# Second context normed in the second mixer, inverse and down products put off, four buffers for the context branch's split weights, later transposes

## The chip, the cores and the metric

The kernel runs on one core of one Trainium2 chip. The metric is the device time of one execution in microseconds (us), as a median over runs. TensorE (PE) multiplies matrices, VectorE (DVE), ScalarE (ACT) and GpSimd (POOL) do the elementwise work, SyncE (SP) issues most of the transfers and POOL the rest; each of these engines works through its own instructions in a fixed order.

## What is computed

`first_block` runs two layers over 256 latent tokens `x` and 256 context tokens `ctx` of 1024 channels, and `second_block` runs a hyena layer and an attention layer over the resulting latent tokens and over a second context `ctx_2`. All matrices are fp32, and nearly all weights are used once. Cut to what matters here:

```
for l in range(2):                      # first_block
    mod   = silu(c) @ w_ada[l] + b_ada[l]          # 6 vectors per stream
    x     = x + gt1 * (token_mixer(norm(x)) @ w_out[l])
    x     = x + gt2 * expert_choice_ffn(norm(x))   # 16 experts, 32 tokens each:
                                                   # (silu(xs@w_gate) * (xs@w_up)) @ w_down
    # ctx the same, in layer 0 alone
for s, t in ((x_lat, c), (ctx_2, c_ctx_2)):        # second_block, layer 0: hyena
    sh, sc, gt = split(silu(t) @ ada_w_2[0] + ada_b_2[0], 3)
    h = rms_norm(s) * (1 + sc) + sh
    x0, x1, v, z = h @ hy_w_in                     # x0, x1, v through a short conv
    u = x1 * v
    y = (irfft(rfft(u) * rfft(k)) + u * d) * x0    # long convolution
    s = s + gt * ((y * silu(z)) @ hy_w_out)
x = x + gt * attention(norm(x), norm(ctx_2))       # layer 1, modulated by ada_w_2[1]
```

## The kernel before

The kernel is written in a tile language whose scheduler decides the order of the instructions on each engine from the order of the code, the dependences and the number of buffers of each tag. The program passes through these stages, in the times of the profiled execution: mixer 0 and routing (0 to 400 us), the 16 experts of layer 0 (to 880), mixer 1 (to 1101; its inner core ends at 1046 and its output projection, on the tiles `mhi` and `mlo`, follows), routing of layer 1 (to 1140), then the 16 experts of layer 1 with the hyena layer of the second context beside them, and from 1835 the latent hyena (to 2080) and attention (to 2365).

**Weights and splitting.** A weight comes in tiles of 1 MB. Expert weights (`ew`) and the modulation weights (`ada`) are used as they are. The weights of projections and of the hyena layer are split by `split` into a high part `hi` (a CAST on ACT) and a low part `lo` (a subtraction on DVE), 512 columns at a time, and each product is made of three matmuls (`mm3`, L109 to L111: hi by hi, lo by hi, hi by lo). `hi` and `lo` have `self.sbufs` buffers each, 2 until the latent hyena.

**Modulation.** `ada` computes the modulation vectors (PE L191; columns L198) from weight tiles of 1 MB that rotate through the five `W` buffers. A table `PLACES` says at which place of the program which step stands, so "1" is w_ada of layer 1 and "a" and "b" are ada_w of the second block's two layers; a place that is in `EVERY` puts its steps between pieces of the mixer's core (`beside`), and the others run their steps in one go.

**Experts of layer 1.** Each of the 16 experts has 12 tiles of 1 MB (four each of gate, up and down), 192 in all, 16 matmuls each (PE L823, inputs `XS` for gate and up, `hT` for down). The first six go to a tag `W2` of their own, the others to the `W` buffers. An expert runs gate, up, `h` (ACT L851, DVE L854), transposes of `h` (L857), down, and `Y` (DVE L869).

**Context hyena.** It stands behind the experts in the code with PSUM of its own, and the scheduler interleaves the two. The context `ctx_2` is loaded, normed and transposed (PE L244) into `hyx`. Then 15 blocks of 128 channels follow (the 16th comes after the step `between`). A block has two weight tiles `Wb` (POOL issues them, two buffers), four projections of 8 by 3 matmuls on `hyx`, convolutions (ACT L1048, DVE L1049 to L1053), a sum and difference `uf` on POOL (L1058) and its transposes on PE (L1059, copied to `u`), a forward transform (`psm<-u,fe`, L1017), the product with the filter `Kt` on DVE (`Yf`, L1075 to L1077), an inverse transform (`ptp<-fi,Yf`, L1017), the product `x0s` (DVE L1088), and its split into `hmh` and `hml`. After every four blocks the output projection (`out_proj`) runs on `hmh` and `hml`.

## Time and profile before

| | |
|---|---|
| median of 3 runs | 2364.46 us (2359.9 to 2367.83) |
| profiled execution | 2366.99 us, span 2365.2 us |
| granted TensorE clock, mean | 0.955 |
| PE busy | 2135.7 us (90%) |
| DVE, ACT, POOL busy | 53%, 31%, 8% |
| DMA | 664.09 MB, mean 281 GB/s |

The span is the profiled time from the first to the last instruction. A busy share is a mean over the whole span, and the stages have different limits, so it says little about one stage. Idle time of an engine that is not the bottleneck costs nothing. A row that names a releaser ("<-DVE lo") says what ended the idle time ahead of the instruction.

### The profile page before, as it was taken

Reading aid. Unit: us, or ns where it says so; the run is one execution under the profiler, and the core shown is the slowest. Engines: PE = TensorE matmul, PEld = TensorE weight load, DVE = VectorE, ACT = ScalarE, POOL = GpSimd, SP = SyncE. Lnnn points to the kernel's source line nnn. Section 1 sums busy time; section 2 is a strip of 40 time slices with the busy share of each in tenths; the row PEclk is TensorE's granted clock in tenths of the full one; section 3 lists DMA queues with packets and bytes.
Section 4 is the critical chain, followed back from the end, with each engine's and each line's share of the span. In section 5 each row is a group of like instructions: output and inputs, shape, how many; then the busy total and the mean of one; then the engine's idle time right before and its main releaser. Section 6 shows DMA issues by size and latency. Waiting matters only on the chain.

```text
span 2365.2 us, 35049 instructions
## 1 busy us (share of the span) xinstructions
PE 2135.7 (90%) x13966; PEld 1436.1 (61%) x13966; DVE 1250.4 (53%) x2533; ACT 737.5 (31%) x1414; POOL 187.7 (8%) x315
## 2 busy tenths in 40 slices
PE   5999988999999989998799998898777999999998
PEld 3776664343343436864376766665234999979786
DVE  3954444333433337654355555544125878875776
ACT  3323331000000014343233222222013555555665
POOL 1000000011010100000011011100001110100100
PEclk8999999999999999999899999998777999999999
DMA  8247545999999996459799999988996545435320
GB/s 342 99 157 312 204 184 193 413 415 415 414 413 415 414 405 251 137 194 370 295 351 365 372 374 370 351 336 327 421 421 262 185 144 188 168 132 189 126 81 26
DMA packets 129588, 664.09 MB, mean 281 GB/s; under 512 B 12666, under 2 KB 23429, under 8 KB 62352
## 3 DMA queue, kind: packets, MB, share of 16 engines
q1 hardware_dynamic: 115616, 602.89, 66.0%
q0 software_dynamic: 13808, 58.96, 6.6%
q8 instruction: 110, 1.80, 0.3%
q14 instruction: 54, 0.44, 0.1%
HBM read 656.56 MB, written 5.24 MB: 280 GB/s over the span
## 4 chain that ended last, share of the span: by engine, by line
PE 72%; DVE 9%; issue 8%; DMA 7%; ACT 3%; POOL 1%; SPq 0%; DVEq 0%; POOLq 0%; ACTq 0%
PE pmm L823 16%; PE pmm L109 12%; PE pmm L111 11%; PE pmm L110 11%; PE pad L191 3%; PE psm L875 2%; DMA W<-in_w_e_gate 1%; DVE lo L105 1%; DMA W<-in_w_e_up 1%; PE ptp L1017 1%; DMA W<-in_w_ada 1%; PE pmm L798 1%; PE pad L978 1%; DMA W<-in_ada_w 1%; PE ppo L1247 1%
## 5 line engine op out<-in xcount | busy, mean ns | idle before, releaser
L823 PE MATMUL pmm<-W,XS 128*32 128x256 f32 (+1 forms) x3040 | 378.8, 478 | 39.7 <-DMA W<-in_w_e_gate 20.3
L105 DVE TENSOR_TENSOR lo<-W,hi 128x512 fp32r<-128x512 f32 (+1 forms) x420 | 283.7, 680 | 187.1 <-ACT hi L104 184.2
L104 ACT CAST hi<-W 128x512 fp32r<-128x512 f32 (+1 forms) x420 | 255.5, 612 | 352.0 <-PE pmm L110 162.9
L823 PEld LDWEIGHTS pmm<-W,XS 128*32 128x32 f32 (+1 forms) x3040 | 127.0, 123 | 241.3 <-issue 151.1
L823 PE MATMUL pmm<-W,hT 128*32 128x256 f32 (+1 forms) x1536 | 190.1, 483 | 20.2 <-DVE hT L101 8.3
L111 PE MATMUL pmm<-hyx,lo 128*128 128x256 f32 x640 | 191.6, 299 | 10.6 <-DVE lo L105 10.6
L109 PE MATMUL pmm<-hyx,hi 128*128 128x256 f32 x640 | 193.4, 302 | 4.8 <-ACT hi L104 4.8
L110 PE MATMUL pmm<-hyx,hi 128*128 128x256 f32 x640 | 185.8, 290 | 0.0
L105 DVE TENSOR_TENSOR lo<-Wb,hi 128x512 fp32r<-128x512 f32 x160 | 109.4, 692 | 117.3 <-ACT hi L104 116.3
L104 ACT CAST hi<-Wb 128x512 fp32r<-128x512 f32 x160 | 96.8, 619 | 209.4 <-PE pmm L110 138.3
L869 DVE TENSOR_TENSOR Y<-pmm,gt 32x512 f32<-32x512 f32 (+1 forms) x128 | 70.9, 554 | 143.5 <-PE pmm L823 141.8
L109 PE MATMUL pmm<-hyl,hi 128*128 128x256 f32 x512 | 144.5, 283 | 1.7 <-DVE rtmp L697 1.7
L110 PE MATMUL pmm<-hyl,hi 128*128 128x256 f32 x512 | 144.1, 282 | 0.0
L111 PE MATMUL pmm<-hyl,lo 128*128 128x256 f32 x512 | 143.1, 283 | 0.0
L109 PEld LDWEIGHTS pmm<-hyx,hi 128*128 128x128 f32 x640 | 126.6, 198 | 23.7 <-ACT hi L104 16.6
L111 PEld LDWEIGHTS pmm<-hyx,lo 128*128 128x128 f32 x640 | 126.3, 197 | 22.3 <-DVE lo L105 14.1
L823 PEld LDWEIGHTS pmm<-W,hT 128*32 128x32 f32 (+1 forms) x1536 | 65.6, 125 | 117.6 <-issue 68.6
L110 PEld LDWEIGHTS pmm<-hyx,hi 128*128 128x128 f32 x640 | 126.6, 198 | 2.4 <-issue 2.2
L851 ACT ACTIVATE h<-pmm 128x256 f32<-128x256 f32 (+1 forms) x31 | 15.1, 488 | 362.1 <-PE pmm L823 361.9
L191 PE MATMUL pad<-W,cpad 128*32 128x512 f32 x576 | 91.0, 643 | 21.6 <-DMA W<-in_w_ada 16.7
L854 DVE TENSOR_TENSOR h<-h,pmm 128x512 f32<-128x512 f32 (+1 forms) x32 | 17.7, 552 | 171.9 <-ACT h L851 89.5
L109 PEld LDWEIGHTS pmm<-hyl,hi 128*128 128x128 f32 x512 | 97.4, 190 | 3.4 <-issue 1.9
(516 smaller groups left out, 4084.1 us busy)
## 6 DMA issues: line engine op xcount, KB each, us to landing
W<-in_w_e_gate SPq DMA_DIRECT2D x128, 1024.0 KB, 11.2
W<-in_w_e_up SPq DMA_DIRECT2D x128, 1024.0 KB, 11.2
W<-in_w_e_down SPq DMA_DIRECT2D x128, 1024.0 KB, 11.2
W<-in_w_ada SPq DMA_DIRECT2D x48, 1024.0 KB, 6.6
W<-in_hyw SPq DMA_DIRECT2D x32, 1024.0 KB, 5.1
Wb<-in_hyw POOLq DMA_DIRECT2D x30, 1024.0 KB, 8.9
W<-in_ada_w SPq DMA_DIRECT2D x24, 1024.0 KB, 5.2
W<-in_at_w_in SPq DMA_DIRECT2D x16, 1024.0 KB, 5.0
```

What stands on the lines that cost most here:

```text
L104: self.nc.scalar.copy(hi, w)
L105: self.nc.vector.tensor_tensor(lo, w, hi.bitcast(F32), op=OP.subtract)
L109: mm(out, lhsT=l[0], rhs=r[0], start=start, stop=False)
L110: mm(out, lhsT=l[0], rhs=r[1], start=False, stop=False)
L111: mm(out, lhsT=l[1], rhs=r[0], start=False, stop=stop)
L191: nc.tensor.matmul(ps[32 * j:32 * j + 32, :], lhsT=self.cpad[:, blk, k0 + k, :], rhs=wt[:, k, j * 512:(j + 1) * 512], start=(k0 + k == 0), ...
L798: nc.tensor.matmul(ps, lhsT=v, rhs=S[s][:, t], start=(t == 0 and q == 0), stop=(t == 1 and q == 1))
L823: self.nc.tensor.matmul(ps[M * j:M * j + M], lhsT=v, rhs=wt[:, j * N:(j + 1) * N], start=(k == 0), stop=(k == 7))
L869: nc.vector.tensor_tensor(Y[s][32 * r:32 * r + 32, c], py[p0:p0 + 32], gt[s][p0:p0 + 32, c], op=OP.mult)
L875: nc.tensor.matmul(ps, lhsT=SgT[s][:, q, t * 128:(t + 1) * 128], rhs=Y[s][:, n * 512:(n + 1) * 512], start=True, stop=True)
L978: nc.tensor.matmul(ps[:, i, f], lhsT=self.fd[:, t, i * 256 + f * 128:i * 256 + (f + 1) * 128], rhs=ab[:, i, t], start=(t == 0), stop=(t == 1))
L1017: self.nc.tensor.matmul(out, lhsT=l[0], rhs=r[0], start=start, stop=stop)
```

## The change

1. The steps "a1 b0 b1" of `ada` move from the place R1 (routing of layer 1) to L1 (beside the pieces of the second mixer's core). Tiles of the second mixer that had room for both streams have room for the latent one alone.
2. `ctx_2` is loaded, normed and transposed right behind the second mixer, in place of behind the experts.
3. The split weights have four buffers, in place of two, in the context hyena (two again during `between`).
4. In the context hyena a block's inverse transform, the product `x0s` and the output projection are put off until the next block has made `uf` (`pend`, `flush`, `back`). The transposes of `uf` stand behind the third projection, in place of directly behind `uf`. `Yf` and `x0s` get two buffers.
5. With one stream, an expert's down products (`down`, from the transposes of `h` on) are put off until the next expert's gate and up products.
6. `W2` has four buffers in place of six, on the other side of the memory.

```diff
-PLACES = dict(..., L1="", R1="a1 b0 b1")
+PLACES = dict(..., L1="a1 b0 b1", R1="")
...
-        F2.enter_context(self.pool("w2", tags=("W2",)))
+        F2.enter_context(self.pool("w2", "right" if ns == 2 else "left", tags=("W2",)))
...
+        put_off = ns == 1
+        def down(e, hv):
...
+            if put_off and e:
+                down(e - 1, last)
+            last = hv
+            if not put_off:
+                down(e, hv)
+        if put_off:
+            down(15, last)
...
-            r = (self.ecount - 1) % 10 if ns == 2 else 11 - self.ecount
+            r = (self.ecount - 1) % 10 if ns == 2 else 9 - self.ecount
             if ns == 1 and r >= 5:
-                t = self.T([128, 2, 1024], "W2", 6)
+                t = self.T([128, 2, 1024], "W2", 4)
...
-                                pt = self.PT([128, 2, 128])
                                 uf = T([128, 2, 128], "uf", 2)
                                 for c, op in enumerate((OP.add, OP.subtract)):
                                     nc.gpsimd.tensor_tensor(uf[:, c], cv[1][:, :128], cv[1][:, 128:][:, ::-1], op=op)
-                                    nc.tensor.transpose(pt[:, c], uf[:, c], self.ident)
-                                self.put([v[:, :, i * 128:(i + 1) * 128] for v in u], pt)
+                                if not three:
+                                    self.flush()
...
+                        if q == (1 if three else 2):
+                            pt = self.PT([128, 2, 128])
+                            for c in range(2):
+                                nc.tensor.transpose(pt[:, c], uf[:, c], self.ident)
+                            self.put([v[:, :, i * 128:(i + 1) * 128] for v in u], pt)
...
+                self.pend.append(lambda ...: self.back(Y, x0s, m, i0=G * g - g0, blocks[0][1]))
+                if three:
+                    self.flush()
...
                 with self.pool("m1"):
                     self.mixer(1, x, hc, m1[1], m1[0], ada)
+                    c2 = self.load_x("ctx_2", "hc")
+                    a0 = self.modA(b0[1], 1, self.colv["ng", 0], "a1")
+                    X2 = self.modulated(c2, a0, b0[1][:, 0], 1, xh="W", side="left")
...
                     with self.psum("ps2", "right", mm=2, tp=1, sm=1), self.pool("bga"):
                         self.wtag, self.wbufs = "Wb", 2
-                        c2 = self.load_x("ctx_2", "hc")
+                        self.sbufs = 4
                         self.hy_consts(False)
...
+                            self.sbufs = 2
                             self.between(x, X, b0)
+                            self.sbufs = 4
```

The queue of SP at the end of the second mixer, before (`w_ada` and `ada_w` are modulation weights, `w_out` the mixer's output weights, `w_e_up` and `w_e_gate` expert weights):

```order
L186 DMA W<-in_w_ada 128x2048 x8
L320 DMA W<-in_w_out 128x4x512 x4
L186 DMA W<-in_ada_w 128x2x1024 x4
L186 DMA W<-in_ada_w 128x2048 x8
L186 DMA W<-in_ada_w 128x2x1024 x4
L895 DMA W<-in_w_e_up 128x2048
```

The same queue now:

```order
L187 DMA W<-in_w_ada 128x2048 x8
L187 DMA W<-in_ada_w 128x2x1024 x4
L187 DMA W<-in_ada_w 128x2048 x8
L187 DMA W<-in_ada_w 128x2x1024 x4
L321 DMA W<-in_w_out 128x4x512 x4
L906 DMA W<-in_w_e_up 128x2048 x4
```

The 16 tiles of `ada_w` have moved ahead of the four of `w_out`.

PE's rows in the first two experts of layer 1, before, up to the first projection of the context hyena (an expert tile has 8 of the matmuls counted here; `xh` is the normed `ctx_2`):

```order
L823 MATMUL pmm<-W,hT 32x256 x32
L244 MATMUL ptp<-cf,xh 128x128 x4
L244 MATMUL pmm<-cf,xh 128x128 x8
L823 MATMUL pmm<-W,XS_7295 32x256 x8
L244 MATMUL ptp<-cf,xh 128x128 x4
L823 MATMUL pmm<-W,XS_7295 32x256 x8
L823 MATMUL pmm<-W,XS_7296 32x256 x16
L823 MATMUL pmm<-W,XS_7295 32x256 x16
L823 MATMUL pmm<-W,XS_7296 32x256 x16
L857 MATMUL ptp<-cf,h_7617 128x128 x2
L109 MATMUL pmm<-hyx_9621,hi 128x256
```

The same place now, where gate and up of the first expert (8 tiles) are followed by two tiles of the second and the first projection:

```order
L824 MATMUL pmm<-W,XS_7357 32x256 x16
L824 MATMUL pmm<-W,XS_7358 32x256 x16
L824 MATMUL pmm<-W,XS_7357 32x256 x8
L217 MATMUL psm<-adbG,cf 128x512
L844 MATMUL ptp<-cf,h_7544 128x128 x2
L824 MATMUL pmm<-W,XS_7357 32x256 x8
L217 MATMUL psm<-adbG,cf 128x512
L110 MATMUL pmm<-hyx_7188,hi 128x256
```

The transposes of `ctx_2` have left this place, and the context hyena begins after 10 expert tiles where 20 stood ahead of it. Between its first and its last block stand 98 expert tiles now, where there were 113; 84 tiles are left for the time behind it, where there were 59.

DVE's rows at the end of one block of the context hyena and the start of the next, before:

```order
L1075 TENSOR_TENSOR Yf<-psm,Kt 128x256
L1076 TENSOR_TENSOR ht_10218<-psm,Kt 128x256
L1075 TENSOR_TENSOR Yf<-psm,Kt 128x256
L1077 TENSOR_TENSOR Yf<-Yf,ht_10218 128x256
L1076 TENSOR_TENSOR ht_10218<-psm,Kt 128x256
L1077 TENSOR_TENSOR Yf<-Yf,ht_10218 128x256
L1064 TENSOR_TENSOR x0s<-cvz,cv_10172 128x256
L869 TENSOR_TENSOR Y<-pmm,gt 32x256 x4
L1088 TENSOR_TENSOR x0s<-x0s,ptp 128x256
L105 TENSOR_TENSOR hml<-x0s,hmh 128x256
L105 TENSOR_TENSOR lo<-Wb,hi 128x512 x4
```

The same place now:

```order
L106 TENSOR_TENSOR lo<-Wb,hi 128x512
L1092 TENSOR_TENSOR Yf<-Yf,ht_10221 128x256
L106 TENSOR_TENSOR lo<-Wb,hi 128x512 x3
L1091 TENSOR_TENSOR ht_10221<-psm,Kt 128x256
L1092 TENSOR_TENSOR Yf<-Yf,ht_10221 128x256
L1060 SCALAR_TENSOR_TENSOR cv_10267<-pmm,hcv,cv_10267 128x255
L1061 SCALAR_TENSOR_TENSOR cv_10267<-pmm,hcv,cv_10267 128x255
L1060 SCALAR_TENSOR_TENSOR cv_10304<-pmm,hcv,cv_10304 128x255
L1122 TENSOR_TENSOR x0s<-x0s,ptp 128x256
L1061 SCALAR_TENSOR_TENSOR cv_10304<-pmm,hcv,cv_10304 128x255
L1064 TENSOR_TENSOR cv_10267<-cv_10267,cv_10304 128x256
L106 TENSOR_TENSOR hml<-x0s,hmh 128x256
```

The first four `lo` of the next block stood behind `x0s<-x0s,ptp`, which needs the inverse transform; now they stand between the products of `Yf`, and `x0s` stands inside the next block's convolutions.

## Rows read from the trace of the kernel before

**Rows 1.** Windows by stage: length, busy time of each engine, granted clock, DMA share, GB/s.

```profile
1020.00:1040.00 20.00, 19.25 (x142) 16.95 (x142) 14.87 (x60) 13.64 (x42) 0.00 (x0) 1.00 0.32 118
1040.00:1060.00 20.00, 16.86 (x67) 9.19 (x66) 8.83 (x27) 4.77 (x16) 1.84 (x2) 0.83 0.31 105
...
1160.00:1184.00 24.00, 11.27 (x128) 4.25 (x124) 4.67 (x10) 4.31 (x8) 0.00 (x0) 0.78 1.01 421
1184.00:1640.00 456.00, 416.12 (x3724) 309.89 (x3714) 243.02 (x481) 132.07 (x255) 45.36 (x79) 0.96 0.92 355
1640.00:1755.00 115.00, 77.26 (x792) 29.05 (x790) 14.28 (x29) 2.28 (x6) 0.30 (x2) 0.74 1.00 412
1755.00:1800.00 45.00, 38.48 (x326) 25.77 (x326) 27.11 (x50) 13.82 (x25) 2.01 (x3) 0.86 1.02 398
```

**Rows 2.** Windows of PE L823 (expert matmuls, 16 to a tile) in layer 1.

```profile
1139.00:1184.00 45.00, 23.56 (x316) 10.49 (x320) 0.84 0.81 326
1184.00:1633.00 449.00, 117.66 (x1804) 48.22 (x1794) 0.97 0.92 355
...
1640.00:1755.00 115.00, 68.35 (x768) 25.66 (x768) 0.74 1.00 412
1755.00:1800.00 45.00, 12.23 (x192) 5.39 (x192) 0.86 1.02 398
```

**Rows 3.** Waits of PE, 1184 to 1640: total us, times, longest us.

```profile
PE pmm L111 <- DVE lo L105: 10.6, 11, 1.7
PE ptp L1059 <- POOL uf L1058: 7.1, 9, 1.4
PE pmm L110 <- DVE lo L105: 5.7, 3, 2.7
PE pmm L109 <- ACT hi L104: 4.6, 7, 1.5
PE psm L1017 <- ACT u L1011: 2.3, 5, 0.5
PE pmm L823 <- ACT hT L99: 2.1, 3, 0.7
PE ptp L1017 <- DVE Yf L1077: 2.0, 2, 1.4
```

**Rows 4.** Groups of ACT, 1184 to 1640: busy, mean ns, idle before and releasers.

```profile
L104 ACT CAST hi<-Wb 128x512 fp32r<-128x512 f32 x150 | 90.7, 619 | 188.6 <-PE pmm L110 128.8 <-PE pmm L111 45.9 <-DVE lo L105 10.3
...
L104 ACT CAST hmh<-x0s 128x256 fp32r<-128x256 f32 x15 | 6.1, 404 | 30.9 <-DVE x0s L1088 30.8
```

**Rows 5.** Timeline of SP, second mixer: start, length, issues.

```profile
985.27 25.75 SPq L186 DMA_DIRECT2D W<-in_w_ada  x8
1013.18 6.03 SPq L320 DMA_DIRECT2D W<-in_w_out  x4
1044.47 54.33 SPq L186 DMA_DIRECT2D W<-in_ada_w  x16
```

**Rows 6.** Timeline of PE, end of mixer 1 and routing.

```profile
1049.32 2.51 PE L191 MATMUL pad<-W,cpad 128*32 128x512 f32 x8 [2.68 <-DMA W<-in_ada_w]
...
1100.47 0.39 PE L111 MATMUL pmm<-hi,mlo 128*128 128x512 f32 x1
...
1109.22 1.91 PE L191 MATMUL pad<-W,cpad 128*32 128x512 f32 x8
...
1112.13 1.05 PE L198 MATMUL pad<-cf,adbG 64*128 64x4 f32 x8
...
1140.44 2.37 PE L823 MATMUL pmm<-W,XS 128*32 128x256 f32 x40
...
1185.84 0.47 PE L857 MATMUL ptp<-cf,h 128*128 128x128 f32 x1 [0.94 <-DVE h L854]
```

**Rows 7.** Timeline of POOL, start of the context hyena.

```profile
1150.93 1.28 POOL L1042 DMA_DIRECT2D Wb<-in_hyw  x2
```

**Rows 8.** DMA issues of the page, part 6: size, us to landing.

```profile
Wb<-in_hyw POOLq DMA_DIRECT2D x30, 1024.0 KB, 8.9
```

More of the change, by code (lines that the diff above doesn't have):

```diff
@@ L49, in __init__ @@
         self.wgate, self.late = [], {}
+        self.pend = []
     def T(self, shape, tag, bufs=1, dt=F32):
@@ L336, in mixer @@
             for s, src in ((0, hc), (1, x)):
-                xh = self.normed(src, "og" if s else "xh", 1)
+                xh = self.normed(src, ("og" if full else "kT") if s else "xh", 1)
                 self.toT(xh, a1, cols[:, 0], s, xhi[:, :, s * 256:s * 256 + 256], xlo[:, :, s * 256:s * 256 + 256],
@@ L345, in mixer @@
         ott = [0, 1, 2, 3] if full else [2, 3]
+        s0 = 0 if full else 1
         cum = []
@@ L643, in mixer @@
                 for t in range(2):
-                    nc.tensor.matmul(ps, lhsT=fz[:, 2 * s + t, h * 128:(h + 1) * 128], rhs=fw[:, t], start=(t == 0), stop=(t == 1))
+                    nc.tensor.matmul(ps, lhsT=fz[:, 2 * (s - s0) + t, h * 128:(h + 1) * 128], rhs=fw[:, t],
+                                     start=(t == 0), stop=(t == 1))
                 fa = T([128, 512], "t2k", 2)
@@ L1025, in hyena @@
         for g0, wg in blocks:
-            m = self.parts([128, blocks[0][1], 256], "hm", 1, True)
+            m = []
             for g in range(g0 // G, (g0 + wg) // G):
@@ L1032, in hyena @@
                 u = self.parts([128, 2, n], "u", 2, three)
-                x0s = T([128, G, 256], "x0s", G)
+                x0s = T([128, G, 256], "x0s", 2)
                 for i in range(G):
@@ L1071, in hyena @@
                     pu.append(ps)
-                Yf = T([128, 2, 2, n], "Yf", HB["Yf"] if three else 1)
+                Yf = T([128, 2, 2, n], "Yf", HB["Yf"] if three else 2)
                 t1 = T([128, 2, n], "ht1", HB["ht1"] if three else 1)
@@ L1081, in hyena, with flush, back, modulated @@
                     self.split(Yf, *Y)
-                py = self.PT([128, G, 256])
-                for i in range(G):
-                    for q in range(4):
-                        c, f = divmod(q, 2)
-                        self.mmx(py[:, i], [v[:, c, f, i * 128:(i + 1) * 128] for v in Y], [v[:, q] for v in self.fis], q == 0, q == 3)
-                i0 = G * g - g0
-                nc.vector.tensor_tensor(x0s, x0s, py, op=OP.mult)
-                self.split(x0s, m[0][:, i0:i0 + G], m[1][:, i0:i0 + G])
-            self.out_proj(x, A["hy_w_out_2"][0], m, g0, wg, gt, dma, wg - G if three and g0 + wg == 16 else 0)
-    def modulated(self, x, a, b, s, tag="hyx", banks=("tp", "mm"), xh="xh"):
+                self.pend.append(lambda Y=Y, x0s=x0s, m=m, i0=G * g - g0: self.back(Y, x0s, m, i0, blocks[0][1]))
+                if three:
+                    self.flush()
+            self.pend.append(lambda m=m, g0=g0, wg=wg: self.out_proj(x, A["hy_w_out_2"][0], m, g0, wg, gt, dma,
+                                                                     wg - G if three and g0 + wg == 16 else 0))
+            if three:
+                self.flush()
+        self.flush()
+    def flush(self):
+        p, self.pend = self.pend, []
+        for f in p:
+            f()
+    def back(self, Y, x0s, m, i0, width):
+        G = x0s.shape[1]
+        if not m:
+            m += self.parts([128, width, 256], "hm", 1, True)
+        py = self.PT([128, G, 256])
+        for i in range(G):
+            for q in range(4):
+                c, f = divmod(q, 2)
+                self.mmx(py[:, i], [v[:, c, f, i * 128:(i + 1) * 128] for v in Y], [v[:, q] for v in self.fis], q == 0, q == 3)
+        self.nc.vector.tensor_tensor(x0s, x0s, py, op=OP.mult)
+        self.split(x0s, *[v[:, i0:i0 + G] for v in m])
+    def modulated(self, x, a, b, s, tag="hyx", banks=("tp", "mm"), xh="xh", side="right"):
         X = (self.T([128, 8, 256], tag + "0", 1, F32R), self.T([128, 8, 256], tag + "1", 1, F32R))
-        with self.pool("xn", tags=("xh", "xtmp")):
+        with self.pool("xn", side, tags=("xh", "xtmp")):
             self.toT(self.normed(x, xh, 1), a, b, s, *X, banks=banks)
@@ L1340, in run @@
         if True:
-            with self.psum("ps0", mm=4, tp=1, sm=2, ad=1):
+            with self.psum("ps0", sm=2, tp=1, mm=4, ad=1):
                 self.setup()
```

117 lines of the change are left out of this document (57 added, 60 removed).

## The prediction

> **What bounds the kernel now.** I read the windows by stage first. From 1184 to 1640 us the context hyena runs between the expert tiles: PE is busy 416.12 of 456 us at a granted clock of 0.96, and the transfers move 355 GB/s at a share of 0.92. PE sets the pace there. From 1640 on, with the hyena finished, the transfers run at a share of 1.00 and 412 GB/s while PE is busy 77.26 of 115 us: the weights set the pace. The same shows from 1160 to 1184, before the hyena starts (421 GB/s, PE busy 11.27 of 24 us) [rows 1]. So the layer's 192 MB of expert tiles are cheap as long as PE has hyena work beside them, and dear when it has none.
>
> The windows of the expert matmuls alone give the two prices. In the mixed stretch 1804 matmuls, 16 to a tile, take 117.66 us, so a tile takes PE 117.66 / 1804 x 16 = 1.04 us [rows 2]. Outside it, a tile takes its transfer: 1.0486 MB at 421 GB/s is 2.49 us [rows 1]. By the order of PE's instructions 20 tiles stand ahead of the hyena, 113 within, and 59 behind; the windows agree, with 316 matmuls before 1184, 1804 to 1633 and 960 after 1640 (19.75, 112.75 and 60 tiles) [rows 2].
>
> Then the waits of PE inside the mixed stretch: the seven largest are 34.4 us together, and none is for an expert tile. 20.9 us are for `hi` and `lo` (10.6 + 5.7 + 4.6), 7.1 for `uf`, 2.0 for `Yf`, 2.1 for `hT` and 2.3 for `u` [rows 3]. Last, who makes `hi` late: the groups of ACT show that the 150 CASTs are busy only 90.7 us and stood idle 188.6 us, 174.7 of it until PE had finished with a buffer (L110 and L111); and `hmh`, which stands ahead of the next block's CASTs in ACT's order, waits 30.9 us for `x0s`, 2.1 us in each of 15 blocks [rows 4]. So the splits are late because they have two buffers and stand behind the inverse transform, not because ACT is slow.
>
> **The change part by part.**
>
> *The modulation tiles.* SP issues `w_out` at 1013.18 and the first `ada_w` only at 1044.47, with 54.33 us for all 16 [rows 5]; from 1020 to 1060 the transfers run at 118 and 105 GB/s [rows 1]. With `ada_w` ahead, these idle transfers are used, and the wait of 2.68 us for `ada_w` [rows 6] goes. But PE now does some 16 tiles inside the core, before 1046, and about 1.06 us for each (8 matmuls; 2.51 at the lower clock, [rows 6]) puts the core's end off by up to 17 us; `w_out`, now last in the queue, waits for `W` buffers that those tiles hold. What the output projection loses in tiles (about 14 of them between 1049 and 1100, 15 to 18 us) the core gains. I take the projection's end, at 1100.5 [rows 6], as unmoved; bounds -6 (the waits for `ada_w` and the low clock at 1040 to 1060 go) and +6 (`w_out` two to three transfers of 2.49 us late). In routing the last tile (1.91 us) and its columns (1.05 us) go [rows 6]: **-3**. The norm of `ctx_2` costs nothing there: 16 transposes between the output projection's matmuls, ACT and DVE being half idle; uncovered, it would be the 2.5 us or so that its transposes take.
>
> *The start of the hyena.* The first expert matmul, at 1140.44 [rows 6], goes to about 1137.4. POOL issues the first two `Wb` at 1150.93 [rows 7], which land 8.9 us later in the median [rows 8]; but the hyena's first matmul stands behind 20 tiles in PE's order, and the last ten of these come at the transfers' pace. Now ten tiles stand ahead, and these have landed: some 10 x 1.04 = 10.4 us. The first `Wb` must wait until PE has read the first four tiles, whose memory it takes over: 1137.4 + about 5 + 1.3 to issue + 8.9 to land + 1.3 for one split = about 1154. Before, its first projection followed the transposes that start at 1185.84 [rows 6], so at about 1186. The hyena starts **-32** earlier, of which the -3 is a part. Bounds: -38 (`Wb`, 2 MB, lands within 5 us, at 421 GB/s) and -22 (four expert tiles of 2.49 us are ahead of it in the queues).
>
> *The mixed stretch.* It loses 15 tiles, 113 to 98, at 1.04 us: **-15.6**. Of the waits, four buffers and the place of `x0s` behind the next block's first `lo` take away the cause of the 20.9 us for `hi` and `lo`; the later transposes that of the 7.1 us for `uf`; a put-off inverse that of the 2.0 for `Yf`; the put-off `down` that of the 2.1 for `hT`. That is 32.1 us if all goes. New waits can take their place: the put-off inverse keeps `hmh` just ahead of the output projection, `u` now follows the third projection, and the two `Wb` buffers are still two. I take three quarters, **-24**; bounds 0 and -34.4. With fewer gaps the granted clock may rise from 0.96; the full clock would take 4% of 416 us, 17 us; I take **-4**, bounds 0 and -17. The stretch becomes 454 - 15.6 - 24 - 4 = 410 us, from 1154 to about 1564 instead of 1640.
>
> *The tail.* It gains 25 tiles, 10 from the start and 15 from the mixed stretch, at 2.49 us: **+62.3**. That is the price of the change, and it has no cover: PE has nothing else until the last tile is there. In SP's order four transfers of the latent hyena's `Kt`, 1 MB in all, now stand ahead of the last down tile: **+2.5**. The put-off `down` leaves two experts' down products behind the last gate and up, but the last tile is a down tile as before, and what follows it is the same. From the latent hyena on, the order of all engines is the same.
>
> The Trainium skill, page "DMA: Bandwidth & Descriptors", section "Where 436 GB/s comes from", says that the side of the HBM, at about 358 GB/s for each core, binds for transfers from there to SBUF. By that the mixed stretch, at 355, would already be at its limit, and the 25 tiles would cost 73 us in place of 62. The trace disagrees: 421 GB/s between 1160 and 1184, 412 over 115 us [rows 1].
>
> Sum: -32 - 15.6 - 24 - 4 + 62.3 + 2.5 = -10.8. On the profiled execution that is 2366.99 to 2356. The median of the runs shown lies 2.5 us below that execution: **2353.5 us**.
>
> As a check from the other side: in the mixed stretch 98 tiles, 30 `Wb` and 15 `Kt` of 256 KB are 131.75 MB of 1.0486, 138 MB, in 410 us, 337 GB/s; far enough from 421 that PE still sets the pace.
>
> **The rivals.**
>
> *The waits are only exchanged* (slower). The splits then hang on something that stays: two `Wb` buffers, released by the last `lo` and 8.9 us in landing [rows 8], or DVE's order, in which `lo` stands between the products of `Yf`. Then neither -24 nor -4 comes: -32 - 15.6 + 62.3 + 2.5 = +17, 2381 as a median. Against it stands that ACT and DVE waited for PE and not for `Wb` [rows 4]. It decides from the point where less than 10 us of waits and clock together are saved.
>
> *Half of it* (no change). Some 17 us of waits and clock are saved in place of 28, which leaves the sum at 0: 2364.
>
> *All of it goes.* All 34.4 us of waits and most of the 17 us of clock: -32 - 15.6 - 34.4 - 13 + 62.3 + 2.5 = -30, and -6 at the second mixer: about 2328. For it speaks that the mixed stretch has no wait for a transfer; against it that PE's own work between gaps, not the gaps, is 416 of 456 us.
>
> *The second mixer stands still.* 16 modulation tiles through five buffers, each held until PE comes to it in the core: if half of them came one transfer late (8 x 2.49 us) instead of landing under the core's work, the core would lose 20 us more; -10.8 + 20 = +9, median 2374. The idle transfers at 1020 to 1060 [rows 1] speak against it.
>
> **How the numbers follow.** Forecast (two thirds to nine tenths of the waits) 0.50; all of it 0.08; half of it 0.20; exchanged 0.15; the mixer's loss 0.07. A measurement of this kernel can tell about 0.3%, 7 us, from no change. The forecast's own range, 2342 to 2362, lies mostly below 2357.4 (0.42 of its 0.50), so faster is 0.42 + 0.08 + a fourth of "half of it", 0.55; slower is 0.13 from "exchanged" and 0.05 from the mixer, 0.18; the rest, 0.27, is the same. The range reaches toward "all of it" and "exchanged" until a tenth is left out at either end: 2332 to 2380.
>
> **What would show it.** Right: the first `hyx` matmul near 1154; the mixed stretch near 410 us, with `hi`, `lo` and `uf` together below 10 us in PE's waits; a stretch at about 415 GB/s of some 200 us behind it; the same spans from the latent hyena on. Wrong: new waits for `Wb`, `hmh` or `u` of 20 us and more in the mixed stretch; the projection of the second mixer ending later than 1107; or a tail with tiles dearer than 2.5 us.

## The result, and the profile after

| | changed | before |
|---|---|---|
| median of 4 runs | 2383.9 us (2380.16 to 2385.69) | 2362.96 us (2359.9 to 2367.83) |
| profiled execution | 2385.67 us | 2366.99 us |
| granted clock, DMA | 0.948, 664.09 MB | 0.955, 664.09 MB |

The ratio is 1.0079 [1.0064, 1.0094]: the change makes the kernel 0.8% slower. The forecast was 2353.5 us, and its range ended at 2380.

The windows of the changed kernel by stage (window, length, busy time of PE, PEld, DVE, ACT and POOL, granted clock, DMA share, GB/s): second mixer to the projection's end, routing, opening, mixed stretch, tail.

```profile
1000.00:1115.00 115.00, 110.77 (x580) 68.32 (x581) 56.48 (x147) 43.82 (x101) 4.19 (x7) 0.94 0.73 272
1115.00:1152.00 37.00, 21.61 (x86) 13.96 (x85) 21.74 (x55) 11.70 (x18) 2.57 (x5) 0.77 0.39 151
1152.00:1171.00 19.00, 14.43 (x169) 6.36 (x168) 1.11 (x2) 5.18 (x9) 2.12 (x4) 0.83 0.77 300
1171.00:1589.00 418.00, 393.49 (x3456) 300.66 (x3456) 235.19 (x470) 125.04 (x248) 45.59 (x79) 0.97 0.92 347
1589.00:1810.00 221.00, 153.83 (x1529) 65.84 (x1527) 41.56 (x84) 12.35 (x26) 1.76 (x5) 0.78 1.01 413
```

The same view of the kernel before, at the bounds that the stages had there:

```profile
1000.00:1101.00 101.00, 96.17 (x519) 59.31 (x517) 48.84 (x132) 36.93 (x89) 3.29 (x5) 0.97 0.68 251
1101.00:1140.00 39.00, 27.42 (x131) 15.82 (x131) 22.26 (x58) 11.48 (x18) 0.90 (x2) 0.82 0.80 328
1140.00:1186.00 46.00, 30.64 (x347) 13.47 (x346) 10.13 (x21) 10.66 (x20) 5.09 (x9) 0.83 0.84 336
1186.00:1643.00 457.00, 418.06 (x3734) 311.25 (x3734) 242.52 (x481) 131.01 (x253) 45.36 (x79) 0.97 0.92 354
1643.00:1792.00 149.00, 107.90 (x1090) 51.97 (x1088) 34.42 (x67) 11.83 (x24) 2.31 (x5) 0.78 1.01 416
```

Read them by length: the opening falls from 46 to 19 us and the mixed stretch from 457 to 418, but the second mixer grows by 14 us and the tail by 72. Then read them by transfers. A stretch's **idle transfer time** is its length times (1 - GB/s / 421): in the mixed stretch 457 x (1 - 354/421) = 73 us before and 418 x (1 - 347/421) = 73 now, in routing 39 x (1 - 328/421) = 9 before and 37 x (1 - 151/421) = 24 now. In both kernels about 278 MB arrive between 1000 us and the last expert matmul, 660 us at 421 GB/s; what differs is the idle time, 133 us before and 147 now. That is 14 of the 18 us by which the last expert ends later, and by this account none of it lies in the mixed stretch. The account is a sum and names no cause: with the same bytes to fetch, a kernel that takes longer must show more idle transfer time. It tells where to look.

The expert matmuls of the changed kernel (windows of PE L824), mixed stretch and tail; 96 tiles within at 101.67/96 = 1.06 us, 86 tiles behind at 2.57 us each:

```profile
1171.00:1589.00 418.00, 101.67 (x1536) 40.71 (x1536) 0.97 0.92 347
1589.00:1810.00 221.00, 124.06 (x1376) 44.65 (x1376) 0.78 1.01 413
```

The waits of PE in the mixed stretch of the changed kernel (total us, times, longest), which answer to [rows 3], and then the CASTs of ACT there, which answer to [rows 4]:

```profile
PE ptp L1078 <- POOL uf L1068: 8.9, 9, 2.6
PE pmm L112 <- DVE lo L106: 5.1, 6, 1.3
PE ptp L1028 <- DVE Yf L1092: 3.0, 2, 2.3
PE ptp L844 <- DVE h L883: 2.3, 3, 1.0
PE psm L1028 <- ACT u L1022: 1.6, 4, 0.5
PE pmm L110 <- ACT hi L105: 1.3, 3, 0.6
```

```profile
L105 ACT CAST hi<-Wb 128x512 fp32r<-128x512 f32 x146 | 83.2, 618 | 67.0 <-PE pmm L111 39.7 <-PE pmm L112 23.6 <-DVE rtmp L698 2.8
```

The splits behave as foreseen: the CASTs' idle time falls from 188.6 to 67.0 us and the waits for `hi` and `lo` from 20.9 to 6.4. The wait for `uf` does not go; it grows from 7.1 to 8.9. PE's own work became shorter as well. Two of its groups in the mixed stretch (busy, mean ns, idle before), of the kernel before and then of the changed one:

```profile
L109 PE MATMUL pmm<-hyx,hi 128*128 128x256 f32 x480 | 146.7, 306 | 2.7 <-ACT hi L104 2.7
L1017 PE MATMUL ptp<-fi,Yf 128*128 128x256 f32 x120 | 34.1, 408 | 3.2 <-DVE Yf L1077 2.0 <-issue 1.2
```

```profile
L110 PE MATMUL pmm<-hyx,hi 128*128 128x256 f32 x480 | 142.6, 298 | 0.8 <-ACT hi L105 0.8
L1028 PE MATMUL ptp<-fi,Yf 128*128 128x256 f32 x120 | 31.2, 389 | 3.6 <-DVE Yf L1092 3.0 <-PE pmm L824 0.6
```

The granted clock is 0.97 in both rows of windows above, but summed from the trace's clock records the lower level holds for 31.8 us of the stretch before and for 24.2 now.

PE's timeline in the changed kernel: end of the output projection, first transposes of routing, first expert matmul, first matmul of the context hyena, and the last expert tile:

```profile
1114.65 0.40 PE L112 MATMUL pmm<-hi,mlo 128*128 128x512 f32 x1
1120.75 0.45 PE L245 MATMUL ptp<-cf,xh 128*128 128x128 f32 x1 [5.70 <-DVE xh L725]
...
1152.08 2.37 PE L824 MATMUL pmm<-W,XS 128*32 128x256 f32 x40
...
1171.11 0.58 PE L110 MATMUL pmm<-hyx,hi 128*128 128x256 f32 x1
...
1807.74 1.94 PE L824 MATMUL pmm<-W,hT 128*32 128x256 f32 x16 [4.40 <-DMA W<-in_w_e_down]
```

The projection ends at 1115.1, not at 1100.9 [rows 6]. What PE does more before it shows in its groups (busy, mean ns, idle before), the changed kernel from 1000 to 1114 and then the kernel before to 1101:

```profile
L192 PE MATMUL pad<-W,cpad 128*32 128x512 f32 x176 | 30.0, 600 | 0.6 <-DVE adbC L201 0.6
...
L217 PE MATMUL psm<-adaG,cf 128*128 128x512 f32 x4 | 3.7, 1038 | 0.0
L245 PE MATMUL ptp<-cf,W 128*128 128x128 f32 x8 | 2.2, 425 | 0.0
...
L245 PE MATMUL pmm<-cf,W 128*128 128x128 f32 x8 | 1.0, 272 | 0.0
```

```profile
L191 PE MATMUL pad<-W,cpad 128*32 128x512 f32 x144 | 23.2, 612 | 3.2 <-DMA W<-in_ada_w 3.2
...
L216 PE MATMUL psm<-adaG,cf 128*128 128x512 f32 x4 | 2.1, 619 | 0.0
```

Four modulation tiles (32 matmuls) have come here from routing, where they ran beside the wait for the norm; there PE now shows 5.70 us of plain wait. And SP's queue of the changed kernel:

```profile
1014.01 48.04 SPq L187 DMA_DIRECT2D W<-in_ada_w  x16
1062.53 9.04 SPq L321 DMA_DIRECT2D W<-in_w_out  x4
1083.66 24.19 SPq L906 DMA_DIRECT2D W<-in_w_e_up  x4
...
1113.71 46.20 SPq L906 DMA_DIRECT2D W<-in_w_e_gate  x8
```

Only nine expert tiles (four `W2`, five `W`) can be fetched ahead of the first expert where there were eleven, and the modulation tiles no longer fill routing's transfers: 151 GB/s.

### The profile page after: what moved, and what is told of

Read it like the earlier page. It is cut to its first block, busy times and chain, and to the rows that moved or that the text cites. A ratio compares the mean times of both kernels' runs of the same rounds, so it can differ in the third digit from the quotient of the medians.

```text
span 2383.9 us, 34944 instructions
## 1 busy us (share of the span) xinstructions
PE 2153.2 (90%) x13955; PEld 1441.7 (60%) x13966; DVE 1248.0 (52%) x2533; ACT 733.7 (31%) x1414; POOL 186.1 (8%) x315
## 2 busy tenths in 40 slices
DMA packets 129587, 664.09 MB, mean 279 GB/s; under 512 B 12666, under 2 KB 23429, under 8 KB 62352
## 5 line engine op out<-in xcount | busy, mean ns | idle before, releaser
L824 PE MATMUL pmm<-W,XS 128*32 128x256 f32 (+1 forms) x3040 | 390.0, 494 | 38.8 <-DMA W<-in_w_e_gate 23.4
L824 PEld LDWEIGHTS pmm<-W,XS 128*32 128x32 f32 (+1 forms) x3040 | 129.3, 126 | 252.1 <-issue 166.0
L824 PE MATMUL pmm<-W,hT 128*32 128x256 f32 (+1 forms) x1536 | 193.9, 483 | 41.1 <-DMA W<-in_w_e_down 31.9
L824 PEld LDWEIGHTS pmm<-W,hT 128*32 128x32 f32 (+1 forms) x1536 | 64.5, 124 | 140.9 <-issue 72.9
L105 ACT CAST hi<-Wb 128x512 fp32r<-128x512 f32 x160 | 91.3, 618 | 86.9 <-PE pmm L111 42.4
```

The lines of the kernel that those rows point to most:

```text
L105: self.nc.scalar.copy(hi, w)
L824: self.nc.tensor.matmul(ps[M * j:M * j + M], lhsT=v, rhs=wt[:, j * N:(j + 1) * N], start=(k == 0), stop=(k == 7))
```

## The experiments

Each edit is made in the changed kernel. The table gives for each kernel the ratio to the kernel before on the same chip; the first expert matmul, the first and last time of the context hyena's blocks ahead of the step `between`, and the last expert matmul (us, profiled execution); the expert tiles ahead of, beside and behind the hyena by PE's order; and the idle transfer time up to the projection's end from 1000 us, in routing, and in the mixed stretch.

| kernel | ratio [95%] | expert | hyena | last | tiles | idle |
|---|---|---|---|---|---|---|
| before | | 1140 | 1186-1643 | 1792 | 20/113/59 | 41, 9, 73 |
| changed | 1.0079 [1.0064, 1.0094] | 1152 | 1171-1589 | 1810 | 10/96/86 | 41, 24, 73 |
| e13 changed again | 1.0069 [1.0045, 1.0093] | 1148 | 1167-1584 | 1804 | 10/96/86 | 38, 23, 72 |
| e2 last step in routing | 1.0069 [1.0049, 1.0088] | 1150 | 1169-1576 | 1803 | 10/94/88 | 41, 24, 69 |
| e5 norm alone back | 1.0020 [1.0009, 1.0031] | 1144 | 1183-1596 | 1796 | 18/96/78 | 34, 24, 69 |
| e3 norm and steps back | 0.9989 [0.9978, 1.0000] | 1143 | 1183-1592 | 1788 | 19/96/77 | 42, 8, 64 |
| e6 norm in routing | 1.0006 [0.9993, 1.0020] | 1144 | 1160-1614 | 1794 | 10/112/70 | 41, 18, 67 |
| e12 e3 with four W2 | 0.9973 [0.9962, 0.9984] | 1140 | 1178-1581 | 1783 | 18/95/79 | 41, 13, 59 |
| e1 two split buffers | 0.9993 [0.9981, 1.0005] | 1148 | 1163-1612 | 1788 | 10/113/69 | 38, 23, 59 |
| e7 put-off alone | 0.9978 [0.9966, 0.9990] | 1142 | 1182-1629 | 1785 | 19/114/59 | 40, 9, 58 |
| e10 inverse alone | 0.9945 [0.9927, 0.9962] | 1137 | 1181-1622 | 1774 | 20/112/60 | 37, 9, 61 |
| e11 down alone | 1.0010 [0.9999, 1.0021] | 1140 | 1181-1633 | 1791 | 19/113/60 | 40, 9, 67 |
| e8 nothing put off | 1.0030 [1.0021, 1.0040] | 1150 | 1167-1575 | 1797 | 10/94/88 | 38, 23, 67 |
| e14 down in place | 1.0015 [1.0004, 1.0026] | 1149 | 1166-1570 | 1793 | 10/94/88 | 40, 24, 61 |
| e15 four buffers, inverse | 0.9974 [0.9960, 0.9987] | 1144 | 1183-1584 | 1787 | 17/94/81 | 43, 13, 64 |
| e16 two buffers, inverse | 1.0057 [1.0036, 1.0078] | 1141 | 1178-1645 | 1803 | 17/112/63 | 39, 13, 83 |
| e4 paced | 1.0056 [1.0037, 1.0075] | 1150 | 1169-1638 | 1806 | 10/117/65 | 38, 23, 71 |
| e9 two products | 0.9898 [0.9877, 0.9920] | 1147 | 1165-1541 | 1763 | 10/95/87 | 38, 24, 34 |

**The second mixer and routing: e2, e5, e3, e6.** In e2 only the last modulation step returns to routing, in the code.

```diff
-L1="a1 b0 b1", R1=""
+L1="a1 b0", R1="b1"
```

> The changed kernel with the last step of the modulation (b1, four tiles of ada_w) back in the routing of layer 1; the norm of ctx_2 stays in the second mixer. Theory (cover): these four tiles ran in routing while the norm of the latent stream was made and cost nothing there; back there, the output projection of the second mixer ends 4 to 7 us earlier than 1114, the wait of 5.7 us for the norm goes, and the first expert comes 4 to 7 us earlier than 1152. Two more tiles in the tail take 3 us of it back: 2379 to 2383. Rival (norm of ctx_2): the loss comes from its transposes and splits between the projection's matmuls, and the first expert still comes at 1152.

The median, 2379.47 us, is within what was expected, but the edit did not do what it was to test. PE still works through all 176 modulation matmuls between 1000 us and the projection's end, and none in routing, where the wait of 5.70 us for the norm is still there:

```profile
L192 PE MATMUL pad<-W,cpad 128*32 128x512 f32 x176 | 30.4, 601 | 1.1 <-DMA W<-in_ada_w 1.1
...
1118.34 0.45 PE L245 MATMUL ptp<-cf,xh 128*128 128x128 f32 x1 [5.70 <-DVE xh L725]
```

The first expert begins at 1149.8, within the spread of the other kernels with the changed mixer (1147 to 1152). So e2 does not tell what the cover of these four tiles was worth, and no other run moves them alone.

e5 takes the load, the norm and the transposes of `ctx_2` back behind the experts and leaves the modulation where the change has it; e3 takes the modulation steps back as well, and `W2` to its six buffers.

```diff
 # e5 and e3
     self.mixer(1, x, hc, m1[1], m1[0], ada)
-    c2 = self.load_x("ctx_2", "hc")
-    a0 = self.modA(b0[1], 1, self.colv["ng", 0], "a1")
-    X2 = self.modulated(c2, a0, b0[1][:, 0], 1, xh="W", side="left")
...
     self.wtag, self.wbufs = "Wb", 2
+    c2 = self.load_x("ctx_2", "hc")
...
+    X2 = self.modulated(c2, a0, b0[1][:, 0], 1)
 # e3 alone
-L1="a1 b0 b1", R1=""
+L1="", R1="a1 b0 b1"
-    t = self.T([128, 2, 1024], "W2", 4)
+    t = self.T([128, 2, 1024], "W2", 6)
```

> The changed kernel with the norm of ctx_2 back behind the experts; all modulation steps stay in the second mixer's core. It prices the norm's share of the 12 us that the second mixer lost. Theory (both): the norm's transposes and splits are 4 us and the four tiles that ran under routing's cover 6 to 7 us, so the first expert comes at about 1146 to 1148, between the 1152 of the change and the 1143 of the kernel with both undone; the rest goes as there (18 tiles ahead, 96 beside, 78 behind), so 2360 + 4 = 2364, between 2361 and 2369. Rival (tiles alone): the first expert still comes at 1150 or later, and the time is 2368 to 2374. Rival (norm alone): the first expert comes by 1144, and the time is 2358 to 2362.

> The changed kernel with the modulation steps, the norm of ctx_2 and the six W2 buffers as before; four split buffers and everything put off stay. Theory: the first expert comes at 1140 again, the hyena starts at about 1186, 96 tiles stand beside it (39 us shorter than before: 18 us for 17 tiles, 20 us of waits and clock), and 77 behind it in place of 59 (18 x 2.49 = 45 us): 2364 + 45 - 39 = 2370, between 2365 and 2380. Rival (mixer is all): the whole loss is the second mixer's 12 us and the rest gains, so the time is at or below 2360.

e5 takes 2370.32 us, a little more than its theory allowed; its first expert comes as the rival (norm alone) had it, its time does not. The first expert begins at 1143.9 in e5 and 1142.8 in e3. The idle transfers up to the first expert are 65 us in the changed kernel, 58 in e5 and 50 in e3. So the norm costs about 7 us of transfers and the modulation steps together with the smaller `W2` about 8, although the steps do use idle transfers in the mixer (34 there, against 42): routing pays them back (24, against 8). The rival of e3, that the front carries the loss, held.

e6 puts the norm and the steps into routing's wait, with two split buffers.

```diff
-L1="a1 b0 b1", R1=""
+L1="", R1="a1 b0 b1"
...
+def fill():
+    ada("R1")
+    c2 = self.load_x("ctx_2", "hc")
...
+r = self.route_tokens(1, [(1, x)], m1[1], m1[0], fill)
...
-self.sbufs = 4
+self.sbufs = 2
```

> The changed kernel with two split buffers, the modulation steps back in routing, and the norm of ctx_2 right behind them, still in routing, where PE waits 4.8, 1.5 and 1.1 us for the choice of tokens. 10 tiles stand ahead of the hyena, 112 beside, 70 behind. Theory: the first expert comes at 1141 to 1144, as in the kernel before, and the rest takes the 640 us that the kernel with two buffers took, so the last expert ends at 1781 to 1784 in place of 1792: 2350 to 2358. Rival: the norm lengthens routing as it lengthened the mixer (first expert at 1148 or later), and the time is 2360 or more.

The theory missed: the median is 2366.65 us. The first expert begins at 1144.1, as the theory had it, and the hyena earliest of all, at 1160; but routing's transfers are idle for 18 us where they were for 9, and the kernel gains only against the changed one. Its mixed stretch has 16.8 us of waits for `uf`.

**The four buffers and the put-off parts: e1, e7, e10, e11, e8, e14, e12, e15, e16.** e1 gives the context hyena its two split buffers back, and nothing else.

```diff
-self.sbufs = 4
+self.sbufs = 2
```

> The changed kernel with two buffers for the split weights of the context branch again. Theory (tiles): with two buffers 113 expert tiles stand beside the hyena and 69 behind it, with four 96 and 86. The tail loses 17 x 2.49 = 42 us, the mixed stretch gains 17 x 1.04 = 18 us and the waits for hi and lo, some 14 us, and 4 us of clock: 6 us less than the changed kernel, about 2378, between 2370 and 2384. Rival (waits): the four buffers are what the change gains, so without them the mixed stretch is 20 us longer with no return, and the time is 2390 or more.

Both theories missed: two buffers are faster than four here. The hyena takes longer (449 us against 418), but with 113 tiles beside it in place of 96, and its transfers are less idle:

```profile
1163.30:1612.20 448.90, 417.74 (x3736) 306.67 (x3739) 239.61 (x477) 129.83 (x252) 43.99 (x79) 0.98 0.94 366
```

e7, e10 and e11 start from the norm and the steps back, six `W2` and two split buffers. e7 keeps both put-off parts, e10 the inverse alone, e11 the down products alone.

```diff
 # e10
-put_off = ns == 1
+put_off = False
 # e11
-if three:
-    self.flush()
+self.flush()
-if q == (1 if three else 2):
+if q == 1:
```

> The kernel before with the put-off inverse and down products and the later transposes alone: two split buffers, six W2 buffers, modulation and norm as before. 19 tiles ahead of the hyena, 114 beside, 59 behind. Theory: the tiles stay where they were, so only the waits count; with two buffers and everything put off PE waited 32.6 us beside the hyena in place of 39, and the stretch took 449 us in place of 457, so 2364 - 8 = 2356, between 2352 and 2361. Rival: what is put off gives nothing by itself, 2362 to 2367.

> The kernel before with the put-off inverse and the later transposes alone (two split buffers, six W2 buffers, modulation and norm as before, down products not put off). 20 tiles ahead, 112 beside, 60 behind. Theory: the inverse is what made putting off pay there (-6 us, with both), so 2358 to 2362; one tile more in the tail takes 1 to 2 us of it. Rival: it is the down products, 2364 to 2368.

> The kernel before with the put-off down products alone (two split buffers, six W2 buffers, modulation and norm as before, inverse and transposes in their old places). 19 tiles ahead, 113 beside, 60 behind. Theory: PE's waits for hT and h are 3 to 4 us beside the hyena and about the same behind it, where a transfer is waited for anyway: 2362 to 2367. Rival: the down products carry the gain of both, 2356 to 2361.

e7 (2359.94 us) came out as its theory had it, e11 (2367.1) at its theory's upper end, and e10 (2350.17) below all that was expected. The put-off inverse, with the later transposes, is the good part of the change: e10 is faster than both kernels, and the fastest of all but e9, which leaves work out. The put-off down products gain nothing alone (e11) and take back more than half of what the inverse gains (e7). e10's mixed stretch has the tiles of before but one in 16 us less:

```profile
1181.00:1622.00 441.00, 412.00 (x3722) 306.29 (x3724) 241.24 (x480) 130.10 (x253) 45.15 (x79) 0.98 0.93 363
```

e8 undoes both put-off parts and the place of the transposes, e14 the down products alone, both with the changed mixer and four buffers.

```diff
 # e8 and e14
-put_off = ns == 1
+put_off = False
 # e8 alone
-if three:
-    self.flush()
+self.flush()
-if q == (1 if three else 2):
+if q == 1:
```

> The changed kernel with nothing put off: down products, inverse transform, output projection and transposes stand where they stood; four split buffers and the second mixer as changed. 10 tiles ahead, 94 beside, 88 behind. Theory: putting off saves some 8 us of waits, and two more tiles in the tail cost 3 us, so 2384 + 11 = 2395, between 2388 and 2402. Rival: the buffers alone took the waits away and putting off adds nothing, 2380 to 2387.

> The changed kernel with the down products not put off, all else as changed. 10 tiles ahead, 94 beside, 88 behind. Theory (down costs): with two buffers and the mixer as before, putting off the inverse alone gave -13 us, with the down products -5, and the down products alone +2, so they cost some 5 to 8 us, and this kernel takes 2372 to 2379. Rival: what is put off and the buffers don't matter once the early norm sets the start, 2380 to 2388.

Both are faster than the changed kernel, and than expected: with four buffers the put-off down products cost time, and the put-off inverse gains little (1.0015 for 1.0030, intervals that touch). No run moves the transposes without the inverse, so the two are not told apart.

e12 is e3 with four `W2` buffers, e15 is e12 with the down products in place, e16 is e15 with two split buffers.

```diff
 # e12: e3, but
-    t = self.T([128, 2, 1024], "W2", 6)
+    t = self.T([128, 2, 1024], "W2", 4)
 # e15: e12, and
-put_off = ns == 1
+put_off = False
 # e16: e15, and
-self.sbufs = 4
+self.sbufs = 2
```

> The kernel with modulation and norm as before, four split buffers and everything put off, and W2 with four buffers in place of six. 18 tiles ahead, 95 beside, 79 behind. Theory (transfers): two tiles fewer can be fetched ahead of the first expert, so the transfers idle some 5 us longer in routing, and the time is 5 us above the 2360 of the same kernel with six: 2362 to 2368. Rival: the buffers are refilled in time either way, 2358 to 2362.

> Modulation, norm and down products as before; four split buffers, four W2 buffers, inverse put off and transposes later. 17 tiles ahead, 94 beside, 81 behind. Against the kernel with the down products put off too (2357.6): 8 us less if these cost as much with four buffers as with two, 2348 to 2353; the rival, that they cost nothing there, gives 2355 to 2361.

> The same with two split buffers: 17 tiles ahead, 112 beside, 63 behind. It is the fastest kernel so far (2350, with six W2 buffers) with four W2 buffers. Theory: 18 tiles that stay beside the hyena and the waits for hi and lo weigh about the same, and two W2 buffers more or less did nothing, so 2348 to 2354, no different from the kernel with four buffers. Rival: the 18 tiles are worth 27 us and the waits 13, so it is 10 us or more below the one with four.

e12 (2357.56 us) and e15 (2357.01) came out near their rivals. The smaller `W2` leaves routing 5 us more idle (13 against 8) and costs no time in e12. e12 is also the changed kernel with the norm and the steps put back and nothing else, and e15 is e14 with the same two put back. That one edit gains 1.0% in the first pair, more than the whole loss of the change, and 0.4% in the second. In the first pair the idle transfers fall by 11 us up to the first expert (65 to 54) and by 14 in the mixed stretch (73 to 59), which this edit does not touch.

e16 fits neither theory: it differs from e10 by `W2` alone (its number and its side of the memory) and is 1.1% slower. Its first expert stands at 1140.7 (1136.5 in e10); its mixed stretch takes 467 us (441 in e10) for the same 112 tiles, idle 83, with waits of PE that e10 does not have (`uf` 0.9 us there):

```profile
PE ptp L1078 <- POOL uf L1068: 18.8, 14, 2.9
PE ptp L1028 <- DVE Yf L1092: 6.9, 6, 1.6
```

**What the mixed stretch is worth: e4 and e9.** e4 holds a block's weights back until an expert's `h` is made, so that as many tiles stay beside the hyena as before the change.

```diff
+if ns == 1 and 0 < e < 14:
+    self.flags[e] = hv[0:1, 0:1]
...
+elif not three and q == 0:
+    e = max(0, (8 * (ct - 1) + 6) // 12)
+    if e in self.flags:
+        self.after(wt[0:1, 0, 0, 0:1], self.flags.pop(e))
```

> The changed kernel with a gate in front of a block's first Wb (a copy of one element of an expert's h by POOL), at about eight expert tiles to a block. 117 tiles now stand beside the hyena and 65 behind it. Theory (tiles): the tail loses 21 x 2.49 = 52 us, the mixed stretch gains 21 x 1.04 = 22 us of tiles and keeps its short waits, so 2384 - 30 = 2354; with gates that hold the hyena up, to 2368. Rival (transfers): the transfers are the limit in the mixed stretch too, at 347 GB/s and a share of 0.92, so that the added tiles cost 2.49 us there as well, PE waits for expert weights within it, and the time stays at 2380 to 2390.

117 tiles stay beside it, and the tail falls from 221 to 168 us; but the mixed stretch grows from 418 to 468, because the pacing makes waits of its own:

```profile
PE pmm L111 <- ACT hi L106: 12.5, 6, 5.8
PE pmm L825 <- DMA W<-in_w_e_gate: 8.8, 3, 4.4
```

The time lies between the theories: the trade can be moved, and moving it alone gains little.

e9 takes PE work out of the mixed stretch. It leaves out part of the computation: the product of the high weight part and the low input part (480 matmuls beside the experts) in the context hyena's projections.

```diff
-self.projT(ps, wt[:, q % 2], X, 0, 256)
+self.projT(ps, wt[:, q % 2], X, 0, 256, short=not three)
```

> The changed kernel with one of the three products (hi weight by low part of the input) left out in the projections of the context hyena, so a third of their matmuls, some 145 us of PE, is not computed. 95 tiles stand beside the hyena, 87 behind it, and the bytes are the same. Theory (transfers): from 1000 us to the last expert 265 MiB must come, 660 us at 421 GB/s, and the changed kernel spends 147 us more than that, 73 of them beside the hyena; less PE work can at most take those 73, since 95 tiles, 30 Wb and 15 Kt need 321 us there. The time falls by 50 to 75 us, to 2310 to 2335, and PE waits for expert weights beside the hyena. Rival (PE alone): the whole 145 us goes, 2240. Rival (chain of a block): convolution, splits and transforms in their order set the pace of a block, and the time falls by less than 30 us.

```profile
1165.00:1541.00 376.00, 338.75 (x2963) 244.49 (x2966) 235.52 (x470) 124.12 (x248) 43.64 (x79) 0.96 0.98 383
```

PE is busy 55 us less (393 to 339), not 145. The 145 us add up rows that overlap; in the changed kernel these matmuls start 0.12 us apart while each row is 0.28 us long, and 480 x 0.12 is 58 us:

```profile
1205.41 0.28 PE L110 MATMUL pmm<-hyx,hi 128*128 128x256 f32 x1
1205.53 0.28 PE L111 MATMUL pmm<-hyx,hi 128*128 128x256 f32 x1
1205.64 0.28 PE L112 MATMUL pmm<-hyx,lo 128*128 128x256 f32 x1
```

The stretch is 42 us shorter with the tiles beside it nearly the same (95 for 96), so the idle transfers fall from 73 to 34 us, and the median from 2383.9 to 2340.19. That is less than the theory's 50 to 75 us and more than the last rival's 30. PE does not come to wait for expert weights, as the theory had it: its longest waits there are for `lo` (10.9 us), `Yf` (8.2) and `uf` (5.5). So PE and its waits for the other engines set the pace of this stretch, and here a hyena made shorter did make the kernel shorter.

**The changed kernel again: e13**, unaltered.

> The changed kernel itself, unaltered, beside the two that follow, so that they stand against it on the same chip: 2380 to 2388 if its 21 us are its own; nearer 2375 if part of it, such as the granted clock of 0.97 beside the hyena where three other kernels with four buffers had 1.00, belonged to its earlier executions.

It agrees in time and tiles, but its projection ends at 1110.5 where the first profile has 1115.1. The granted clock up to there is 0.98, where the first profile has 0.94. A single milestone carries some 5 us of doubt, so sixteen of the kernels are better read in two groups: with the steps and the norm in the mixer (the changed kernel, e13, e1, e2, e4, e8, e9, e14) the projection ends between 1109.5 and 1115.1, with both as before (the kernel before, e3, e7, e10, e11, e12, e15, e16) between 1097.4 and 1104.6. The means are 10.4 us apart.

## Why the prediction was wrong

The last expert matmul ends 18.0 us later (1791.7 to 1809.7), and what follows is unchanged. By the prediction's own steps:

| step | predicted | measured |
|---|---|---|
| projection's end | 0 (bounds ±6) | +14.2 (1100.9 to 1115.1; +9.6 in e13) |
| routing | -3 | -2.5 (39.5 to 37.0) |
| opening, first expert to hyena | -29 | -26.7 (45.7 to 19.0) |
| mixed stretch | -15.6 - 24 - 4 = -44 | -39.2 (457.2 to 418.0) |
| tail | +62.3 + 2.5 = +65 | +72.3 (148.3 to 220.6) |
| sum | -10.8 | +18.1 |

**The step that failed** is the one on the modulation tiles: "I take the projection's end ... as unmoved", with the norm of `ctx_2` "costs nothing there". It is 14 of the 29 us of error. The prediction moved the tiles by a balance between core and projection, took 14 of the 16 to have stood in the projection and "the last tile" in routing. PE's rows have 12 in the projection (96 matmuls) and four in routing: 8 matmuls at 1109.22 [rows 6] and 24 ahead of them, where they were covered by the wait for the norm:

```profile
1102.49 5.34 PE L191 MATMUL pad<-W,cpad 128*32 128x512 f32 x24 [0.83 <-DVE adbC L200]
```

In a stretch where PE is busy 111 of 115 us, the 6.8 us of these four tiles (30.0 against 23.2), the 3.2 us of the transposes and 1.6 us of slower `psm` rows make 11.6 of the 14.2; the rest is not told apart (the granted clock was 0.94 for 0.97). The pair of profiles lies at the wide end: over the two groups of eight kernels the projection's end moves by 10.4 us, which is still beyond the bound of 6. e12, e3 and e5 confirm the place from the other side: the first expert stands at 1140 in e12 and 1143 in e3, with both undone, and at 1144 in e5, with the norm alone undone, and the front's idle transfers fall from 65 us to 54, 50 and 58. The seven kernels with norm and steps back have 46 to 56 us, the eight with both in the mixer 61 to 65. How the loss is shared between the steps and the norm is not shown, since the fronts of kernels with the same edit differ by as much as 7 us. The prediction's own sign, a projection that ends later than 1107, came in all eight kernels with the changed mixer. The rival on the second mixer had the place right and the reason wrong: not late buffers (PE waited 0.6 us there), but PE itself, and the fetch ahead that ended too early. The rival of exchanged waits named 2381, near what was measured, by luck: it needs less than 10 us of waits and clock saved, and some 18 were.

**The mixed stretch** went as foreseen in its size, -39 for -44. The waits of [rows 3] fell from 34.4 to 19.9 us, counting the same seven, 14.5 for the 24 predicted. The 17 tiles took 17 us of PE with them, 101.67 us (above) for these 118.35 of the kernel before:

```profile
1186.00:1643.00 457.00, 118.35 (x1808) 48.69 (x1808) 0.97 0.92 354
```

The clock gave what was forecast: 7.6 us less at the lower level, and half of that, 3.8, is an estimate of what it saved, for the 4 predicted. That leaves some 4 us that no row here names. The later transposes did not take the wait for `uf` away.

**The tail** was mis-sized by 7 us: 86 tiles stand behind the hyena in the trace, not 84, and they took 2.57 us each for 2.49. With the start it holds 27 tiles more, not 25. The rate did not give out: 413 GB/s over 221 us. The Trainium skill, page "DMA: Bandwidth & Descriptors", section "Where 436 GB/s comes from", puts the limit of such transfers at about 358 GB/s for each core; as in [rows 1], the measurement differs and decides.

**What the sum says, read again.** Seventeen tiles that leave the mixed stretch save 17 x 1.04 us there and cost 17 x 2.49 behind it, 25 us. The hyena net of its tiles became 340 - 318 = 22 us shorter (457.2 - 113 x 1.04, 418.0 - 96 x 1.04). The two cancel, which the idle transfers show at once: 73 us and 73 us. The prediction had this cancelling in it (its own gain from the mixed stretch was only 6 us); what it lacked was the view of the transfers as one account, in which only less idle time counts. By that account four split buffers show no gain as such: mixed stretches with four have 59 to 73 us idle (e9, which leaves work out, aside), those with two (e1, e6, e7, e10, e11, e16) 58 to 83.

**What stays open.** The parts do not add up. Three pairs differ by the number of split buffers alone: two in place of four gain 0.8% from e13 to e1, 0.1% from e3 to e7, where the intervals overlap, and lose 0.8% from e15 to e16. Putting the norm and the steps back gains 1.0% in one pair and 0.4% in another. Six to four `W2` buffers made no loss between e3 and e12 and cost 1.1% between e10 and e16, with waits for `uf` of 18.8 us in one and 0.9 in the other. The put-off down products cost 13 us between e14 and e13 by the ratios, 8 between e10 and e7, nothing between e15 and e12. Each edit reorders the mixed stretch as a whole, and no run here ties these effects of 10 us and more to one cause.

## What to carry to other kernels

Where a layer must fetch a fixed amount, add up by stage the time in which the transfers are not at full rate: an edit gains what that sum loses, and a stall removed beside the weights is only exchanged if the weights then come behind. Work moved into an earlier stage costs its full time if the engine is already full there, and leaves a hole where it had covered a wait; look at both places. Rows of pipelined matmuls overlap, so price work that is to go by the distance of their starts or by the busy time of a window, not by adding up rows (e9). See in the trace that an edit moved what it was to move: in e2 the order of the code changed and the matmuls stayed. When a change has several parts, time them apart: here the put-off inverse, with the later transposes, gains 0.55% alone, and the parts around it lost more than that.

## What the runs showed of the hardware

A short wait of PE in a busy stretch can cost more than itself. From the timeline of PE in the changed kernel:

```profile
1217.87 1.10 PE L1028 MATMUL ptp<-fi,Yf 128*128 128x256 f32 x4 [2.27 <-DVE Yf L1092]
...
1219.65 0.41 PE L110 MATMUL pmm<-hyx,hi 128*128 128x256 f32 x1
...
1225.14 0.28 PE L110 MATMUL pmm<-hyx,hi 128*128 128x256 f32 x1
```

```profile
1216.00:1219.00 3.00, 1.13 (x6) 1.05 (x7) 2.95 (x8) 0.15 (x1) 0.52 (x1) 1.00 0.96 363
1219.00:1222.00 3.00, 3.00 (x16) 3.00 (x16) 1.92 (x4) 0.00 (x0) 0.59 (x2) 0.51 0.73 292
1222.00:1225.00 3.00, 3.00 (x27) 2.04 (x27) 1.12 (x3) 0.93 (x2) 0.00 (x0) 0.92 0.89 268
1225.00:1228.00 3.00, 3.00 (x34) 2.28 (x32) 0.94 (x2) 1.08 (x2) 0.00 (x0) 1.00 1.00 371
```

Behind the wait of 2.27 us the granted clock is 0.51 for three microseconds, the lower level of 1.2 GHz, and PE starts 16 matmuls where it starts 34, partly of other kinds, from 1225 on. By an estimate from these rows, three microseconds at half the rate, the wait of 2.27 us took 1.5 more with it. In the same stretch the clock is 0.51 and 0.50 over three microseconds behind the waits of 2.06 us (1316) and 2.57 us (1429), and 1.00 behind one of 1.30 us (1241). It is 0.50 from 1496 on too, behind two waits of 0.89 and 0.46 us close together, so the length of a single wait does not tell all.
